# Hybrid encoder block on one core: the single unit's first step moved ahead of the second products, and the residual rows' transfers moved to ScalarE's queue

## The chip, the core and the metric

The kernel runs on one core of a Trainium2 chip. The metric is the time of one execution on the device in microseconds; the kernel before takes 1399.41 us, the median of 3 runs (1399.37 to 1400.16). Engine names are those of the profile: PE (TensorE, matmul) and PEld (its weight loads), DVE (VectorE), ACT (ScalarE), POOL (GpSimd) and SP (SyncE, which issues most DMAs); a q behind a name is the engine's sequencer, which issues DMAs and waits.

## The reference, cut to what matters

One encoder layer over 256 tokens of width 2048, everything in float32. Three attention mixers are merged by gates, projected by `w_o` and added to the residual; then comes a gated feed-forward layer of inner width 5632 with a second residual add:

```
h = rms_norm(x, g_mix);  proj = h @ w_in            # q, k, v of the mixers and three gates
...
merged = gates0 * (oa @ w_br_a) + gates1 * (ob @ w_br_b) + gates2 * (oc @ w_br_c)
x = x + merged @ w_o
hf = rms_norm(x, g_ffn) @ w_ffn_in                   # 2048 x 11264
x = x + (silu(hf[..., :D_FF]) * hf[..., D_FF:]) @ w_ffn_out
```

The change touches the `w_o` product, the feed-forward products and the last residual add.

## The kernel before, in words

**Tiling.** The 256 tokens are two halves of 128 rows (t = 0, 1). A weight matrix is cut into blocks of 256 input rows by 512 output columns, 512 KB each, stored so that a block is one DMA of 128 partitions x 1024 values. A float32 product is made from rounded parts: ACT copies a weight tile to the type that PE takes (`whi`, L444 in `halves`), DVE subtracts that from the original to get the remainder (`wlo`, L455 in `low`), and PE does three matmuls of 128x512 for each pair of tiles: high x high, high x low, low x high.

**Seven products instead of eight.** `pair` (L457) makes two neighbouring blocks of 512 output columns at once. Where it can, it takes a 2x2 group (two token halves or input blocks by two column blocks) and replaces its eight block products by seven with sums of blocks as operands. These seven are the steps X, W, P, Y, Q, Z, H, with a digit for the group; the sums of the activations are prepared tiles (`forms`, `lone`), the sums of the weights are made by accumulating DMAs on POOL (L545, L554, L560) or by DVE (L644, L646, L648; L577, L579, L581 for the single unit). Blocks outside such groups are the plain steps d (first column block) and D (second).

**Order.** The order of the steps is written by hand in the `STEPS_` lists (L54 to L65), one string for the front, one for the back and one for the tail of a pair; a "." in a front takes one step of the tail of the pair before. `run` (L681) calls each step's preparation (loads, DVE sums, `whi`, `wlo`) four steps ahead of its matmuls (`ahead` is 4), so that ACT and DVE stand four steps ahead of PE in program order. Letters l, r, a and s are not products: l0 and l1 start the two groups' first loads and the accumulating DMA into `t`; r0 and r1 load the block `b22` of group 0 or 1 (`begin2`, L547); s0 loads the two blocks of the single unit and sums into one of them (L557); a0 and a1 accumulate one more block into `t` (L553).

**Ends of phases.** All X steps of a pair add into one PSUM bank. After the last of them `phase_end` (L601) has ACT copy that bank into a new one for Y (L613); P, the next product, goes on adding into the X bank and so must wait for the copy. After the last W step ACT copies the W bank to `m5` (L616), and after the last P step DVE writes `m5` minus X into the W bank (L618). These copies are put on ACT and DVE in the order in which the products are called (`nc.follow`), that is behind the `whi` copies of the four steps that follow the step which ends the phase.

**The feed-forward pairs.** `feeding` (L1058) makes eleven pairs of `w_ffn` (n = 0 to 10), in three groups (0 to 3, 4 to 7, 8 to 10), each group followed by two pairs of `w_ffn_out`. Pair n = 0 uses `STEPS_FFN0`, the other ten use `STEPS_FFN5`. This list has two groups (0 and 1) and one single unit: S1 to S4 are a 2x2 group inside one input block, of half the width. S1 is half an X product and half a W product, so it belongs to both phases; S2 is P and Y, S3 Q and Z, S4 H. Its plain steps are D4, D5, D7 and d4, d5, d7; the three d steps are its tail and stand at the three "." of the next front.

**Places.** A loaded block goes to the first free place of one list (`free`, L212; 15 places from n = 1 on), and `release` puts a place at the end of that list after the step that uses the block. SP issues loads in program order, so a load waits until the place that it was given is free, and everything behind it on SP waits too.

**Residual rows.** In `projecting` (L997) DVE adds the `w_o` product to the residual rows `x` in SBUF (L1023), and `keep` (L1008) stores each finished block of 128 x 512 to the DRAM tile `held`: eight DMAs of 256 KB on SP, three ticks after the add. Pairs of `w_ffn_out` that aren't the last accumulate into `held` by POOL's DMAs (L1096). Before the last two pairs `rows_back` (L1052) loads `held` into two SBUF tiles `xb0` and `xb1`, two DMAs of 1 MB on SP, eight ticks after it is started; the last additions (L1103) write into these and `store` (L1048) sends them out from SP.

Of the kernel before, what the change touches and what calls it, by code (L numbers as in the profile page):

```python
# [25 lines left out]
NC = 512  # L26
# [32 lines left out]
STEPS_O2 = ("l0 X0 . r0 W0 . P0 Y0 . Q0 .", "Z0 D2 H0 D3 d2 D4 D5 d3 D6 D7", "d4 d5 d6 d7")  # L59
STEPS_FFN0 = ("l0 l1 X0 X1 . r0 W0 . r1 W1 . P0 P1 . Y0 Q0 Q1 Y1", "Z0 Z1 D6 H0 D7 H1 D4 D5", "d6 d7 d4 d5")  # L60
STEPS_FFN = ("l0 l1 X0 X1 . r0 W0 r1 W1 P0 P1 . Y0 Y1 . Q0 Q1 .", "Z0 Z1 D4 H0 D5 H1 D6 D7", "d4 d5 d6 d7")
STEPS_FFN5 = ("l0 l1 s0 X0 X1 . W0 W1 S1 r0 P0 . r1 P1 S2 Y0 Y1 . Q0 a0 Q1 a1 S3",
              "Z0 Z1 D4 H0 D5 H1 D7 S4", "d4 d5 d7")
STEPS_LAST = ("l0 l1 X0 X1 . r0 W0 . r1 W1 . P0 P1 . Y0 Q0 Q1 Y1", "Z0 Z1 H0 H1 D4 D5", "d4 d5")
STEPS_LAST2 = ("l0 l1 X0 X1 . r0 W0 r1 W1 P0 P1 . Y0 Q0 Q1 Y1", "Z0 Z1 D4 H0 D5 H1 d4 d5", "")  # L65
# [40 lines left out]
def encoder_block(ctx: ExitStack, tc: tile.TileContext, a: dict, out: bass.AP):  # L106
    nc = InOrder(tc)
# [13 lines left out]
    def s8(shape, name, dt=F32R, pool=None):  # L121
        return (pool or big).tile(shape, dt, name=name, tag="s8")

    def s4(shape, name, dt=F32):
        return mid.tile(shape, dt, name=name, tag="s4")
# [37 lines left out]
    def row_scale(ss, r):  # L163

        v = small.tile([P, T], F32, name="rs_v")
        nc.follow(nc.vector.tensor_scalar(v, ss, 1.0 / D, EPS, op0=ALU.mult, op1=ALU.add))
        y = []
        yield from root_of(v, [P, T], y)
        nc.follow(nc.vector.tensor_copy(r[:, 0], y[0]))
        nc.follow(nc.vector.tensor_mul(r[:, 1], y[0], y[0]))  # L170
# [14 lines left out]
    def start(steps):  # L185

        job = [0, steps]
        side.append(job)
        advance(job)
# [7 lines left out]
    def urgent(steps):  # L197

        while True:
            with tc.high_priority():  # L200
                try:
                    lag = next(steps)
                except StopIteration:
                    return
            yield lag
# [94 lines left out]
    def transposed(src, dst, g=None, lag=1, also=None, single=None):  # L300


        full = None
        for h in range(2):
            if h:
                yield lag
            tp = bank("tp", "tp")
            for k in range(2):
                for t in range(T):
                    nc.tensor.transpose(tp[:, k * S + t * P:k * S + (t + 1) * P],  # L310
                                        src[t][:, (2 * h + k) * P:(2 * h + k + 1) * P], ident)
            if g is None:
                d = dst(2 * h, 2)
                split(d[0], d[1], tp.rearrange("p (k s) -> p k s", s=S))
            else:
                for k in range(2):
                    d = dst(2 * h + k, 1)
                    split(d[0], d[1], tp[:, k * S:(k + 1) * S], g(2 * h + k))
            if also is not None:
                if full is None:  # L320
                    full = s4([P, 2, 4, P], "ffull")
                to, of = full[:, :, 2 * h:2 * h + 2], tp.rearrange("p (k t s) -> p k t s", t=T, s=P)
                if g is None:
                    nc.scalar.activation(to, of, AF.Copy)
                else:
                    for k in range(2):
                        nc.scalar.activation(to[:, k], of[:, k], AF.Copy, scale=g(2 * h + k))
            if single is not None and h == 0:
                one, of = s4([P, 1, 4, P], "ffull"), tp.rearrange("p (k s) -> p k s", s=S)
                for k in range(2):  # L330
                    nc.scalar.activation(one[:, 0, 2 * k:2 * k + 2].rearrange("p t s -> p (t s)"), of[:, k], AF.Copy,
                                         scale=g(k) if g else 1.0)
                token_sums(one, single)
        if also is not None:
            token_sums(full, also)
# [46 lines left out]
    def hold(n, steps):  # L382
        yield n
        yield from steps
# [554 lines left out]
    held = dram.tile([P, T, D], F32, name="held")  # L939
    mT, x1T, x, room, lone = {}, [], [], [], []  # L940
# [56 lines left out]
    def projecting():  # L997
        def rows():
            yield 16
            for t in range(T):  # L1000
                x.append(s8([P, D], f"x{t}", F32))
                nc.sync.dma_start(out=x[t], in_=a["x"][t * P:(t + 1) * P, :])
                yield 1
        start(rows())
        mTl = lambda k: (mT[k // 4][:, 0, k % 4], mT[k // 4][:, 1, k % 4])
        ended = []

        def keep(i, xc):  # L1008
            for t in range(T):
                nc.sync.dma_start(out=held[:, t, i * NC:(i + 1) * NC], in_=xc[t])  # L1010
            yield 1

        def root():
            yield 4
            ssr = small.tile([P, T], F32, name="ss", bufs=1)
            nc.follow(nc.vector.tensor_reduce(ssr, ss1, axis=AX.X, op=ALU.add))
            yield from row_scale(ssr, r_f)

        for n in (0, 2):
            def add(c, r, n=n):  # L1020
                xc = [x[t][:, (n + c) * NC:(n + c + 1) * NC] for t in range(T)]
                for t in range(T):
                    nc.vector.tensor_add(xc[t], r[t], xc[t])  # L1023
                start(hold(3, keep(n + c, xc)))
                ended.append(n + c)
                last = len(ended) == 4

                def later():
                    yield 1
                    sq = s4([P, T, NC], "sq")  # L1030
                    for t in range(T):
                        nc.scalar.activation(sq[:, t], xc[t], AF.Square, accum_out=ss1[:, t, n + c:n + c + 1])
                    if last:
                        start(urgent(root()))
                    yield 2
                    if not x1T:
                        x1T.extend(s8([P, 2, 4, S], "x1T") for _ in range(4))
                        room.extend(form_room(3))
                        lone.append(s4([P, 1, 2, 4, P], "lone", F32R))
                    yield from transposed(xc, lambda k, m: (x1T[n + c][:, 0, k], x1T[n + c][:, 1, k]),  # L1040
                                          lambda k: gT[:, 2, 4 * (n + c) + k:4 * (n + c) + k + 1], 2,
                                          also=room[2 + n + c] if n == 0 else None,
                                          single=lone[0] if n + c == 3 else None)
                start(urgent(later()))
            yield pair(block_pair(a["w_o"], n), mTl, STEPS_O2 if n else STEPS_O, add, TWO[:1], by_room(lambda: room))
# [6 lines left out]
    def rows_back():  # L1052
        x[:] = [s8([P, D], f"xb{t}", F32) for t in range(T)]
        for t in range(T):
            nc.sync.dma_start(out=x[t], in_=held[:, t])
            yield 1

    def feeding():  # L1058
        for c0, c1 in ((0, 4), (4, 8), (8, KF // 4)):
# [3 lines left out]
            for n in range(c0, c1):  # L1063
# [5 lines left out]
                def hidden(c, v, av=av, n=n - c0, hT=hT):  # L1069
# [8 lines left out]
                    def later():  # L1078
                        tl = hT[n] = s8([P, 2, 4, S], "hT", pool=home(n))
                        yield 3  # L1080
                        yield from transposed([av[0][:, t] for t in range(T)],
                                              lambda k, m: (tl[:, 0, k:k + m], tl[:, 1, k:k + m]), lag=2,
                                              also=room[n] if n < 2 else None)
                    start(urgent(later()))
                yield pair(lambda u, c, n=n: a["w_ffn"][n][2 * u + 1 - c], x1l, STEPS_FFN5 if n else STEPS_FFN0, hidden,
                           TWO, by_room(lambda: room[2:4]), single=(6, lambda f: [lone[0][:, 0, i, (f + 1) % 4] for i in range(2)]))
            pairs = (STEPS_LAST, STEPS_LAST2) if last else (STEPS_FFN, STEPS_FFN)
            if last:
                start(hold(8, rows_back()))
# [111 lines left out]
```

## Time and profile before

| | |
|---|---|
| median of 3 runs | 1399.41 us (1399.37 to 1400.16) |
| the profiled execution | 1397.66 us, of which its span is 1395.9 us |
| granted PE clock over the span | 0.99 |
| busy share of PE, DVE, ACT, POOL | 98%, 83%, 63%, 6% |
| mean DMA rate | 231 GB/s |
| DMA into and out of HBM | 312.37 MB read, 9.17 MB written |

Read it so: a busy share says how much of the span an engine was doing something, not that it ran at its best rate; the granted clock is the share of PE's full clock that the throttle allowed. The view of waits names, for an engine's idle time, which instruction ended it, with the total, the number of times and the longest. The timeline prints for each instruction its start, its duration, engine, line and tiles, and in brackets the idle time of its engine before it. Views by window give busy time, clock and DMA share of one stretch.

### The profile page before, as it was taken

To read this page: it belongs to the slowest core of one execution; us is meant where nothing else is said; L and a number is where in the kernel's file an instruction comes from. 1 tells how busy PE (TensorE), PEld (TensorE's weight loads), DVE (VectorE), ACT (ScalarE), POOL (GpSimd) and SP (SyncE) were. 2 spreads that over 40 slices of the span, in tenths; PEclk is the share of its full clock that TensorE was granted. 3 is DMA by queue.
4 is the path that set the end of the run, shared out by engine and by line. 5 is a ranking of instruction groups with operands and counts; after the bars stand their busy time and mean duration, and the time that the engine had idled before them with its cause. 6 is when DMAs were issued, how large, how long until landed. Compare 5 with 4: busy or idle time off the path is not lost. (4 is left out here: it accounts for less than half of the span.)

```text
span 1395.9 us, 17542 instructions
## 1 busy us (share of the span) xinstructions
PE 1361.7 (98%) x6146; PEld 1121.9 (80%) x6146; DVE 1161.0 (83%) x1460; ACT 885.1 (63%) x1181; POOL 88.2 (6%) x98
## 2 busy tenths in 40 slices
PE   9999999999999999999989999999999999999998
PEld 7888888888888888888767878878777888777877
DVE  6878877779977969867979898977898898878897
ACT  7876665655655656656656666666666666656664
POOL 0010000000000000000000100011100001110000
PEclk9999999999999999999999999999999999999999
DMA  9976445576668558738577976789876888887953
GB/s 372 336 237 207 137 162 168 165 218 196 239 193 300 196 181 294 235 134 294 182 247 257 288 201 214 251 253 289 259 209 230 270 256 263 209 269 232 336 160 107
DMA packets 94282, 322.71 MB, mean 231 GB/s; under 512 B 10545, under 2 KB 13105, under 8 KB 93681
## 3 DMA queue, kind: packets, MB, share of 16 engines
q1 hardware_dynamic: 80928, 280.14, 55.9%
q0 software_dynamic: 13120, 41.42, 16.2%
q8 instruction: 48, 0.79, 0.2%
q14 instruction: 42, 0.34, 0.1%
q10 hardware_dynamic: 144, 0.02, 0.0%
HBM read 312.37 MB, written 9.17 MB: 230 GB/s over the span
## 5 line engine op out<-in xcount | busy, mean ns | idle before, releaser
L444 ACT ACTIVATE whi<-raw 128x1024 fp32r<-128x1024 f32 (+1 forms) x320 | 316.3, 1000 | 200.3 <-PE mmQ L81 37.5
L455 DVE TENSOR_TENSOR wlo<-raw,whi 128x1024 fp32r<-128x1024 f32 (+1 forms) x320 | 364.7, 1150 | 86.8 <-ACT whi L444 84.2
L444 ACT ACTIVATE whi<-both 128x1024 fp32r<-128x1024 f32 (+1 forms) x195 | 194.5, 1006 | 118.6 <-DVE both L644 24.1
L455 DVE TENSOR_TENSOR wlo<-both,whi 128x1024 fp32r<-128x1024 f32 (+1 forms) x195 | 224.6, 1158 | 44.6 <-ACT whi L444 43.2
L81 PE MATMUL mm<-whi,xT 128*128 128x512 f32 x640 | 202.3, 393 | 0.0
L81 PE MATMUL mmX<-whi,forms 128*128 128x512 f32 x368 | 129.6, 407 | 25.4 <-ACT mmY L613 23.9
L81 PEld LDWEIGHTS mm<-whi,xT 128*128 128x128 f32 x640 | 119.2, 188 | 23.5 <-issue 0.4
L135 DVE TENSOR_TENSOR wlo<-raw,whi 128x1024 fp32r<-128x1024 f32 x82 | 103.2, 1261 | 36.9 <-ACT whi L134 36.4
L81 PE MATMUL mm<-wlo,xT 128*128 128x512 f32 x320 | 125.6, 393 | 0.0
L81 PE MATMUL mmW<-whi,forms 128*128 128x512 f32 x368 | 123.9, 392 | 0.0
L455 DVE TENSOR_TENSOR wlo<-more,whi 128x1024 fp32r<-128x1024 f32 (+1 forms) x88 | 103.6, 1178 | 23.7 <-ACT whi L444 22.9
L134 ACT ACTIVATE whi<-raw 128x1024 fp32r<-128x1024 f32 x82 | 86.8, 1062 | 56.0 <-PE mm L81 39.9
L81 PE MATMUL mmX<-whi,x1T 128*128 128x512 f32 x352 | 121.7, 390 | 0.0
L444 ACT ACTIVATE whi<-more 128x1024 fp32r<-128x1024 f32 (+1 forms) x88 | 89.8, 1022 | 43.6 <-PE mmQ L81 8.3
L81 PEld LDWEIGHTS mmX<-whi,forms 128*128 128x128 f32 x368 | 71.3, 194 | 45.1 <-ACT mmY L613 28.1
L81 PE MATMUL mmY<-whi,x1T 128*128 128x512 f32 x244 | 85.5, 407 | 0.2 <-ACT whi L444 0.2
L81 PEld LDWEIGHTS mmW<-whi,forms 128*128 128x128 f32 x368 | 69.1, 188 | 14.1
L81 PEld LDWEIGHTS mmX<-whi,x1T 128*128 128x128 f32 x352 | 66.5, 189 | 14.1
L81 PE MATMUL mmX<-wlo,forms 128*128 128x512 f32 x184 | 74.1, 403 | 0.0
L81 PE MATMUL mmW<-wlo,forms 128*128 128x512 f32 x184 | 71.8, 390 | 0.1
L81 PEld LDWEIGHTS mm<-wlo,xT 128*128 128x128 f32 x320 | 60.2, 188 | 12.4 <-issue 0.7
L81 PE MATMUL mmX<-wlo,x1T 128*128 128x512 f32 x176 | 68.8, 391 | 0.1
(315 smaller groups left out, 2631.1 us busy)
## 6 DMA issues: line engine op xcount, KB each, us to landing
raw<-in_w_ffn SPq DMA_DIRECT2D x85, 512.0 KB, 8.3
both<-in_w_ffn SPq DMA_DIRECT2D x67, 512.0 KB, 8.6
raw<-in_w_gate SPq DMA_DIRECT2D x66, 512.0 KB, 4.7
raw<-in_w_qkv SPq DMA_DIRECT2D x64, 512.0 KB, 4.3
raw<-in_w_ffn_out SPq DMA_DIRECT2D x42, 512.0 KB, 6.2
both<-in_w_ffn_out SPq DMA_DIRECT2D x35, 512.0 KB, 5.7
more<-in_w_ffn SPq DMA_DIRECT2D x24, 512.0 KB, 8.3
both<-in_w_ffn POOLq DMA_DIRECT2D x24, 512.0 KB, 8.7
```

The lines of the kernel that those rows point to most:

```text
L81: ins = op(*args, **kw)
L134: nc.scalar.activation(hi, src, AF.Copy)
L135: nc.vector.tensor_sub(lo, src, hi.bitcast(F32))
L444: nc.follow(nc.scalar.activation(hi[:, o], v, AF.Copy))
L455: nc.follow(nc.vector.tensor_sub(*part))
```

## The change

Two edits. In `STEPS_FFN5`, r0 and r1 move forward, right behind X0 and X1; S1 moves from behind W1 to the place ahead of W0; and the second "." (a tail step of the pair before) moves from behind P0 to between W0 and W1. In `keep` and `rows_back` the DMAs are issued by ACT instead of SP, in program order with the other followed instructions of ACT.

```
-STEPS_FFN5 = ("l0 l1 s0 X0 X1 . W0 W1 S1 r0 P0 . r1 P1 S2 Y0 Y1 . Q0 a0 Q1 a1 S3",
+STEPS_FFN5 = ("l0 l1 s0 X0 r0 X1 r1 . S1 W0 . W1 P0 P1 S2 Y0 Y1 . Q0 a0 Q1 a1 S3",
               "Z0 Z1 D4 H0 D5 H1 D7 S4", "d4 d5 d7")
...
         def keep(i, xc):
             for t in range(T):
-                nc.sync.dma_start(out=held[:, t, i * NC:(i + 1) * NC], in_=xc[t])
+                nc.follow(nc.scalar.dma_start(out=held[:, t, i * NC:(i + 1) * NC], in_=xc[t]))
...
         for t in range(T):
-            nc.sync.dma_start(out=x[t], in_=held[:, t])
+            nc.follow(nc.scalar.dma_start(out=x[t], in_=held[:, t]))
```

No arithmetic changes; the same matmuls, copies and DMAs are made. With the tail steps filled in, the products of a front that follows another `STEPS_FFN5` pair come in this order:

```
before: X0 X1 d4 W0 W1 S1 P0 d5 P1 S2 Y0 Y1 d7 Q0 Q1 S3
after:  X0 X1 d4 S1 W0 d5 W1 P0 P1 S2 Y0 Y1 d7 Q0 Q1 S3
```

## The prediction

> **What bounds the kernel now.** I read the page first, then the view of waits, then the timeline around one wait of the kind that leads it. The page's head and its first line say that PE is the bound:
>
> ```profile
> span 1395.9 us, 17542 instructions
> PE 1361.7 (98%) x6146; PEld 1121.9 (80%) x6146; DVE 1161.0 (83%) x1460; ACT 885.1 (63%) x1181; POOL 88.2 (6%) x98
> ```
>
> Only 1395.9 - 1361.7 = 34.2 us of PE are idle. The waits (total, times, longest) say where:
>
> ```profile
> PE mmX L81 <- ACT mmY L613: 23.9, 10, 5.0
> PE mmX L81 <- DVE mmW L618: 1.5, 1, 1.5
> ```
>
> One wait holds 23.9 us of the 34.2; the next is 1.5. Ten times is once for each `STEPS_FFN5` pair: P0 adds into the X bank and waits until ACT has copied that bank for Y. One of the ten, ACT's timeline first, then PE's:
>
> ```profile
> 1026.95 0.63 ACT L444 ACTIVATE whi<-both 128x512 fp32r<-128x512 f32 x1 [0.68 <-DVE both L577]
> 1027.49 0.61 ACT L444 ACTIVATE whi<-raw 128x512 fp32r<-128x512 f32 x1
> 1028.01 0.58 ACT L613 ACTIVATE mmY<-mmX 128x512 f32<-128x512 f32 x1
> ```
>
> ```profile
> 1026.13 0.39 PE L81 MATMUL mmW<-whi,lone 128*128 128x512 f32 x1
> 1028.64 0.77 PE L81 MATMUL mmX<-whi,forms 128*128 128x512 f32 x1 [2.12 <-ACT mmY L613]
> ...
> 1030.48 0.63 PE L81 MATMUL mmX<-wlo,forms 128*128 128x512 f32 x1
> 1030.91 0.63 PE L81 MATMUL mmX<-whi,forms 128*128 128x512 f32 x1
> ```
>
> PE had finished S1 at 1026.5. The copy takes 0.58 us but starts at 1028.01, because on ACT it stands behind the `whi` copies of four more steps, P0, d5, P1 and S2, and S2's wait for a DVE sum (L577). So PE doesn't wait for a busy ACT; it waits for a place in ACT's order. And the wait costs more than itself: behind it matmuls start 0.43 us apart (1030.48 to 1030.91). Windows of 5 us behind each of the ten waits (columns: PE, PEld, DVE, ACT, POOL busy, then the granted clock, DMA share, GB/s) show why:
>
> ```profile
> 719.70:724.70 5.00, 4.98 (x12) 3.92 (x13) 2.66 (x3) 2.47 (x3) 0.00 (x0) 0.50 0.31 107
> ...
> 1287.80:1292.80 5.00, 5.00 (x15) 3.97 (x16) 2.91 (x4) 2.46 (x3) 0.86 (x1) 0.66 0.44 105
> ```
>
> In seven of the ten the clock is below full: 0.50 once, 0.68 once, 0.66 five times; the other three show 1.00. Lost clock is 5.0 x (0.50 + 0.32 + 5 x 0.34) = 12.6 us. The waits thus cost 23.9 + 12.6 = 36.5 us, of which PE's busy share shows only the first part.
>
> **S1 ahead of W0.** This removes no work; what counts is what stands between S1 and P0 on PE, and on ACT ahead of the copy. Rows of the same pair, DVE and then PE:
>
> ```profile
> 1018.02 1.23 DVE L455 TENSOR_TENSOR wlo<-raw,whi 128x1024 fp32r<-128x1024 f32 x1
> 1019.17 1.22 DVE L455 TENSOR_TENSOR wlo<-both,whi 128x1024 fp32r<-128x1024 f32 x1
> 1020.30 1.22 DVE L644 TENSOR_TENSOR raw<-raw,more 128x1024 f32<-128x1024 f32 x1
> 1021.44 0.69 DVE L455 TENSOR_TENSOR wlo<-raw,whi 128x512 fp32r<-128x512 f32 x1
> ```
>
> ```profile
> 1022.28 0.39 PE L81 MATMUL mmW<-whi,forms 128*128 128x512 f32 x1
> ...
> 1023.64 0.39 PE L81 MATMUL mmW<-whi,forms 128*128 128x512 f32 x1
> ```
>
> A step of six matmuls takes PE 1023.64 - 1022.28 = 1.36 us, a plain step of twelve 2.72. In the new order S1 starts at 1022.28, its X half ends at about 1022.96, and behind it come W half 0.68, W0 1.36, d5 2.72, W1 1.36: P0 would start at 1029.1. The four steps behind S1 are now W0, d5, W1 and P0, so the copy stands behind P0's `whi`. DVE from 1018.02: two halves of S1 (0.60 each, 0.69 long with the overlap that the full ones show), W0 and d5 (1.14 each), P0's sum 1.14: 1022.6. ACT then copies P0's `whi` (1.06) and the X bank (0.58): 1024.3, 4.8 us ahead of P0. I therefore cost the wait at nothing. Its cover is these 6.1 us of PE work; without it the old 2.1 to 5 us are back. The W phase now ends with W1; its copy to `m5` goes behind Y0's `whi`, and its reader (L618) comes only after S2, as before.
>
> What is late next is DVE: three steps with sums (P0, P1, S2) now follow each other with no plain step between. From a window from one copy (L613) to the next:
>
> ```profile
> 982.90:1028.00 45.10, 43.00 (x185) 35.07 (x185) 39.82 (x45) 29.64 (x37) 4.34 (x5) 0.96 0.79 239
> ```
>
> ```profile
> 1008.00 1.23 DVE L455 TENSOR_TENSOR wlo<-raw,whi 128x1024 fp32r<-128x1024 f32 x1 [2.20 <-ACT whi L444]
> ```
>
> Without wait and clock loss PE needs 45.10 - 2.1 - 1.7 = 41.3 us for this interval; DVE is busy for 39.82 and sits 2.20 for H1's block, together 42.0: 0.7 short. Such tight intervals are four or five (those where the sums for `forms` are made as well), and DVE runs 2 to 3 us ahead of PE (below: 2.6), which absorbs most of it. I take 1 us in all, between 0 and 5 x 0.7 = 3.5.
>
> **r0 and r1 behind X0 and X1.** Two loads more stand on SP ahead of d4's, and one more ahead of d5's; S1's blocks are wanted two steps earlier. SP, then landing times by kind (count, KB, median us), then d4 on ACT, DVE and PE:
>
> ```profile
> 1000.09 0.33 SPq L81 DMA_DIRECT2D both<-in_w_ffn  x1
> 1001.23 0.33 SPq L81 DMA_DIRECT2D more<-in_w_ffn  x1
> 1002.36 2.06 SPq L81 DMA_DIRECT2D both<-in_w_ffn  x2
> ```
>
> ```profile
> both<-in_w_ffn SPq DMA_DIRECT2D x67, 512.0 KB, 8.6
> ```
>
> ```profile
> 1013.68 1.06 ACT L444 ACTIVATE whi<-both 128x1024 fp32r<-128x1024 f32 x1 [0.29 <-PE mmX L81]
> ...
> 1015.74 1.22 DVE L455 TENSOR_TENSOR wlo<-both,whi 128x1024 fp32r<-128x1024 f32 x1
> ...
> 1019.56 0.39 PE L81 MATMUL mmY<-whi,x1T 128*128 128x512 f32 x1
> ```
>
> These issues are d4 (1000.09), r0 (1001.23), then d5 and r1 (1002.36 and behind). d4 becomes the third: 1002.36 instead of 1000.09, 2.3 us later. Landing 0.33 + 8.6 later, at 1011.3, it is still 2.4 us ahead of ACT's use at 1013.68, and `wlo` has another 1019.56 - 1016.96 = 2.6 us before PE. Cover 5.0 us: nothing, in most pairs. Not so where loads are late already:
>
> ```profile
> 704.68 1.06 ACT L444 ACTIVATE whi<-raw 128x1024 fp32r<-128x1024 f32 x1 [5.19 <-DMA raw<-in_w_ffn]
> ```
>
> ```profile
> 938.00:983.00 45.00, 43.13 (x189) 35.39 (x189) 36.51 (x38) 28.65 (x35) 5.51 (x6) 1.00 0.89 262
> ```
>
> In the pair n = 1 ACT waits 5.19 us for the tail step d6, and this load falls behind r0 and r1: 2.3 us more, taken in full (0 to 4.6). Behind the first pair of each later group (n = 5, n = 9) the DMA share is 0.89 against 0.79; I take 1 us in each (0 to 2.5). What remains is 1 + 2.3 + 2 = 5.3 us.
>
> **Stores and loads through ACT.**
>
> ```profile
> SPq L81 <- DVE x L1023: 66.6, 8, 21.9
> ```
>
> ```profile
> 570.00:661.00 91.00, 91.00 (x418) 75.30 (x417) 71.23 (x80) 56.75 (x80) 2.58 (x3) 1.00 0.67 231
> ```
>
> ```profile
> 0.74 0.40 ACTq L349 DMA_DIRECT2D gT<-in_g_rows  x1
> ```
>
> The eight stores block SP for 66.6 us until the rows are added, and the weight loads behind them. But in that stage PE is busy for 91.00 of 91 us, so earlier loads win nothing. ACT issues a DMA in 0.40 us (its only one); eight make 3.2 us, in a stage where it is idle for 34 of 91. The added wait, for the add, is queued ahead of ACT's `whi`; the store stands three ticks behind the add, and ACT's squares (L1032) already wait for the same rows, so I cost it at nothing (0 to 8 x 0.4, or -1 where three loads of n = 0 come sooner). `rows_back`:
>
> ```profile
> 1310.60 0.80 SPq L81 DMA_DIRECT2D xb<-held  x2
> ```
>
> ```profile
> 1355.73 0.35 DVE xb L1103
> ```
>
> SP issued them at 1310.60 without any wait; ACT reaches them eight steps (of 1.36 to 2.72 us) later, by my estimate around 1328; even at twice the 8.6 us of a block half as large they land by 1346, 10 us ahead of the first use. Nothing either way.
>
> **Sum.** 36.5 - 5.3 = 31.2 us less. The profiled execution (1397.66, span 1395.9) would be at 1366.5; the median stands 1.75 above it, so 1399.41 - 31.2 = 1368.2.
>
> [...] The rows say that a PE wait of 2.1 us was followed by half clock in this pair. [...]
>
> **Rivals.** *DVE becomes the bound.* For it: 39.82 of 45.10 busy, and of its 5.28 idle only 2.20 is H1's. If another 1.0 of the other 3.08 stays, an interval takes 43.0, 2.1 less than now: ten give 21, so 1378. Against: DVE's lead of 2.6 us, and the intervals without `forms`, in which it can win it back. Chance 0.15. *Nothing moves*, the copy being late behind P0's sum after all: 1399.4. Against: 4.8 us of room. 0.03. *The slow clock stays*: 23.9 - 5.3 = 18.6 less, 1380.8. For it: three waits of the ten have no slow clock behind them; against: seven have, at once. 0.03. *d4's load stops ACT in every pair*, slower: a pair wins 36.5 / 10 = 3.65, so from a landing 5.0 + 3.65 = 8.65 us later than worked out (17.3 us from issue) it loses. At 19 us PE waits 5.4 and the clock costs 1.26 again, 3.0 more than now in each pair: 1429. Against: 8.6 is the median. 0.04.
>
> **How the numbers follow.** The forecast has 0.75. Low end: no residue, and some us of the 34.2 - 23.9 others besides: 1360. High end: the DVE rival with the upper residues of the late loads (5.3 more), 1384; left out are no change, slower, and the worst of the others. A difference under 0.2% (2.8 us) can't be told from none: faster 0.93, same 0.03, slower 0.04.
>
> **What would show it.** Right: PE's wait for L613 gone from the list, no half clock between 715 and 1295, copies 41 to 42 us apart, d6 of n = 1 later on ACT. Wrong: PE waiting for `wlo` (L455) for more than 1 us at P1, S2 or Y0; ACT waiting for `in_w_ffn` at d4; ACT idle ahead of its own DMA issues.

## The result and the profile after

The changed kernel takes 1383.28 us, the median of four runs (1382.37 to 1384.77); the kernel before took 1399.39 us beside it. The ratio is 0.9889, with a 95% interval of 0.9872 to 0.9906. The forecast was 1368.2: the time moved the way it said, by 16.1 us instead of 31.2. The profiled execution took 1383.93 us, of which the span is 1382.2. The head of its page and the first line:

```profile
span 1382.2 us, 17556 instructions
PE 1357.3 (98%) x6146; PEld 1113.1 (81%) x6146; DVE 1157.9 (84%) x1460; ACT 878.1 (64%) x1181; POOL 88.1 (6%) x98
```

PE is idle for 1382.2 - 1357.3 = 24.9 us, 9.3 less than before. Its busy time fell by only 4.4 us, although the granted clock over the span rose from 0.990 to 0.998. PE's waits (total, times, longest):

```profile
PE mmX L81 <- DVE wlo L455: 8.4, 9, 1.3
PE mmW L81 <- DVE wlo L455: 5.3, 11, 0.7
PE mmX L81 <- DVE mmW L618: 2.6, 2, 1.5
PE mmY L81 <- DVE wlo L455: 1.6, 4, 0.8
```

The wait for L613, 23.9 us before, is gone from the list. In its place PE waits for low halves: 8.4 + 5.3 + 1.6 = 15.3 us in 24 short waits, where the kernel before had 2.8 us in five (0.7, 0.9 and 1.2 in the same three rows). The copy itself, on ACT, and the first matmul of P0, on PE, in the pair n = 6:

```profile
1014.90 1.06 ACT L444 ACTIVATE whi<-raw 128x1024 fp32r<-128x1024 f32 x1 [2.69 <-DVE raw L644]
1015.87 0.58 ACT L613 ACTIVATE mmY<-mmX 128x512 f32<-128x512 f32 x1
```

```profile
1019.40 0.39 PE L81 MATMUL mmX<-whi,forms 128*128 128x512 f32 x1
```

The copy ends at 1016.45, 2.95 us ahead of P0 (4.8 were forecast); it stands behind P0's `whi`, as worked out. From one copy to the next (columns: PE, PEld, DVE, ACT, POOL busy, then granted clock, DMA share, GB/s):

```profile
972.50:1015.90 43.40, 41.90 (x184) 33.17 (x183) 39.52 (x45) 28.72 (x38) 4.34 (x5) 1.00 0.84 252
1015.90:1059.60 43.70, 41.78 (x187) 33.73 (x186) 39.50 (x45) 28.78 (x37) 4.32 (x5) 1.00 0.84 246
```

The clock is full, but the interval is 43.4 to 43.7 us where 41 to 42 were forecast. DVE is busy for 39.5 of it (39.8 before). Where its other 4.2 us went, on ACT and then on DVE, in the second of these windows:

```profile
1042.84 1.06 ACT L444 ACTIVATE whi<-more 128x1024 fp32r<-128x1024 f32 x1 [6.22 <-DMA more<-in_w_ffn]
```

```profile
1038.76 1.21 DVE L455 TENSOR_TENSOR wlo<-raw,whi 128x1024 fp32r<-128x1024 f32 x1
1043.93 1.23 DVE L455 TENSOR_TENSOR wlo<-more,whi 128x1024 fp32r<-128x1024 f32 x1 [3.96 <-ACT whi L444]
```

This is H1: ACT waits 6.22 us for the block that a1 accumulates, and DVE 3.96 us for ACT, nearly all of DVE's idle time in this window. The same instruction in the kernel before:

```profile
1052.86 1.22 DVE L455 TENSOR_TENSOR wlo<-both,whi 128x1024 fp32r<-128x1024 f32 x1 [1.96 <-ACT whi L444]
```

Added up over the ten `STEPS_FFN5` pairs, DVE's idle time ahead of H1's low half was 17.2 us before (0.13 to 4.51 each) and is 30.5 after (0.52 to 4.26): 13.3 us more.

**The round that sets the interval.** After Q1's sum (L646), which still reads the block `t`, a1 may be issued on POOL; its landing lets ACT make H1's `whi`, then DVE makes H1's low half, and then comes all DVE work up to the next Q1 sum. POOL's rows for the pair n = 6, after and then before:

```profile
1029.27 0.86 POOL L545 DMA_DIRECT2D both<-in_w_ffn  x1 [2.92 <-ACT whi L444]
1029.81 1.21 POOL L554 DMA_DIRECT2D more<-in_w_ffn  x1
```

```profile
1038.99 0.86 POOL L545 DMA_DIRECT2D raw<-in_w_ffn  x1 [2.76 <-DMA raw<-in_w_ffn]
1039.53 1.21 POOL L554 DMA_DIRECT2D both<-in_w_ffn  x1
```

L545 is the accumulating load of the next pair's l1, L554 is a1, right behind it on the same queue in both kernels. After the change a1 lands at 1042.7, 12.9 us after its issue; before it took 12.1. The view of line L554, before and then after (a0 and a1 together):

```profile
  ACT whi L444: 31.3, 11
...
DMA to landing us min/median/max: 5.4/10.6/13.8
```

```profile
  ACT whi L444: 55.9, 16
...
DMA to landing us min/median/max: 8.3/12.1/14.2
```

Over the ten a1 loads the time from issue to landing adds up to 118.7 us before (10.3 to 13.8 each) and 131.9 after (12.6 to 14.2), 13.2 us more; their issue comes 1.3 us later behind Q1's sum, in all. So nearly all of DVE's 13.3 us come from the longer landing, not from a later issue. The traces' records of issue and landing say where it is longer. In both kernels a1 lands 3.6 to 4.7 us after the last of the DMAs that were issued ahead of it. The time from a1's issue until that last one has landed adds up to 79.7 us before and 92.2 after, 12.5 us more. The growth is in the loads that are still on their way when a1 is issued.

### The profile page after: what moved, and what is told of

The parts are those of the page before. It is cut to its first block, busy times and chain, and to the rows that moved or that the text cites. A ratio compares the mean times of both kernels' runs of the same rounds, so it can differ in the third digit from the quotient of the medians.

```text
span 1382.2 us, 17556 instructions
## 1 busy us (share of the span) xinstructions
PE 1357.3 (98%) x6146; PEld 1113.1 (81%) x6146; DVE 1157.9 (84%) x1460; ACT 878.1 (64%) x1181; POOL 88.1 (6%) x98
## 4 chain that ended last, share of the span: by engine, by line
PE 71%; DVE 13%; DMA 11%; issue 3%; ACT 3%; POOL 0%; SPq 0%; ACTq 0%; DVEq 0%; POOLq 0%
PE mmX L81 19%; PE mm L81 16%; PE mmW L81 14%; PE mmY L81 10%; PE mmQ L81 8%; DVE wlo L455 8%; DMA both<-in_w_ffn 7%; ACT whi L444 2%; DMA more<-in_w_ffn 2%; DVE raw L646 1%; PE o L81 1%; PE sc L81 1%; DMA raw<-in_w_ffn_out 1%; DVE both L646 1%; PE tp L81 1%
## 5 line engine op out<-in xcount | busy, mean ns | idle before, releaser
L444 ACT ACTIVATE whi<-both 128x1024 fp32r<-128x1024 f32 (+1 forms) x194 | 190.5, 992 | 110.6 <-DMA both<-in_w_ffn 34.0
L455 DVE TENSOR_TENSOR wlo<-both,whi 128x1024 fp32r<-128x1024 f32 (+1 forms) x194 | 220.2, 1141 | 40.6 <-ACT whi L444 39.7
L81 PE MATMUL mmX<-whi,forms 128*128 128x512 f32 x368 | 123.4, 395 | 2.6 <-DVE mmW L618 2.6
L134 ACT ACTIVATE whi<-raw 128x1024 fp32r<-128x1024 f32 x82 | 86.8, 1061 | 57.8 <-PE mm L81 41.3
L81 PE MATMUL mmY<-whi,x1T 128*128 128x512 f32 x244 | 81.5, 390 | 0.3 <-ACT whi L444 0.3
```

What stands on the lines that cost most here:

```text
L81: ins = op(*args, **kw)
L134: nc.scalar.activation(hi, src, AF.Copy)
L444: nc.follow(nc.scalar.activation(hi[:, o], v, AF.Copy))
L455: nc.follow(nc.vector.tensor_sub(*part))
```

## The experiments

Theory A: the round over a1's landing sets the interval, so the gain went into H1's wait. Rivals: DVE's work as a whole sets it, wherever it stands; the moved transfers cost it; or nothing in particular does. Each diff is against the changed kernel except where it says otherwise, and each ratio is against the kernel before, timed on the same chip. The changed kernel's is 0.9889; a ratio lower by 0.001 is 1.4 us.

**The two parts of the change, each alone.** First the new order with the residual rows on SP as before:

```
-                nc.follow(nc.scalar.dma_start(out=held[:, t, i * NC:(i + 1) * NC], in_=xc[t]))
+                nc.sync.dma_start(out=held[:, t, i * NC:(i + 1) * NC], in_=xc[t])
...
-            nc.follow(nc.scalar.dma_start(out=x[t], in_=held[:, t]))
+            nc.sync.dma_start(out=x[t], in_=held[:, t])
```

> The changed kernel with the stores and loads of the residual rows back on SP; only the order of the steps is changed. Theory A (what is left is DVE: 39.5 us of work an interval plus about 4 us in which it waits for H1's block, the accumulating DMA a1): the two queues play no part, so 1383 us, within 3 of the changed kernel, and ACT waits 5 to 6 us for H1's block as there. Rival C (ACT pays for issuing the residual DMAs): 5 to 10 us faster than the changed kernel, 1373 to 1378.

Measured: 1385.73 us (1384.93 to 1387.28), ratio 0.9922 (0.9906 to 0.9939). Then the reverse of this diff put into the kernel before:

> The kernel before with only the residual rows' DMAs on ACT. Theory A: nothing is gained or lost where PE is full, 1399 us within 3, with the ten waits for L613 as before. Rival C: slower than the kernel before by 5 to 10 us, 1404 to 1409.

Measured: 1396.66 us (1393.28 to 1399.89), ratio 0.9986 (0.9972 to 1.0). The order makes nearly all of the gain. The queue part gives about 2 us by itself, which its interval (up to 1.0) does not tell from none, and 2.5 (by the ratios 4.6) with the new order. One place where it shows: from the copy of n = 0 to that of n = 1 the time is 57.3 us with SP and 54.5 with ACT (54.5 to 56.5 in the other kernels with this front and ACT's queue), and ACT's wait for d6 of n = 1 is 7.92 us with SP and 5.99 with ACT. SP's 66.6 us of waits for the added rows (67.5 in the order-only run) are gone with ACT's queue, so a likely reason is that the loads of n = 0 no longer stand behind the stores; no run separates this.

**H1 behind D7.** H1 gets the 2.7 us of D7's matmuls more:

```
-               "Z0 Z1 D4 H0 D5 H1 D7 S4", "d4 d5 d7")
+               "Z0 Z1 D4 H0 D5 D7 H1 S4", "d4 d5 d7")
```

> The changed kernel with H1 one step later, behind D7. Theory A: DVE does D7's remainder (1.14 us) and its neighbours inside the wait for a1, so the interval shrinks by 1.1 to 2.3 us in eight of the ten pairs: 9 to 18 us faster than the changed kernel, 1365 to 1374, and DVE's idle time ahead of H1's remainder falls from 4 to 2 us or less. Rival B (r0 and r1 ahead of d4's load are what is lost): no difference, 1383 within 3.

Measured: 1371.53 us (1371.31 to 1373.7), ratio 0.9822 (0.9807 to 0.9836), 9 us (by the ratios) to 12 us (by the medians) less than the changed kernel. From copy to copy, the same two intervals:

```profile
969.92:1011.17 41.25, 40.82 (x184) 33.48 (x183) 39.71 (x45) 28.82 (x38) 4.34 (x5) 1.00 0.87 268
1011.17:1052.99 41.82, 41.36 (x186) 33.93 (x186) 39.82 (x45) 28.75 (x38) 4.32 (x5) 1.00 0.85 258
```

These are close to the 41.3 us that the prediction gave as PE's need. The work is the same (DVE 39.7 to 39.8); only the idle time went: 9.1 us ahead of H1 in ten pairs, instead of 30.5. The rows also show that PE's busy share hides part of such a loss: the same 184 matmuls at full clock count as 41.90 us busy in the changed kernel and as 40.82 here.

**r0 and r1 back at the second products.**

```
-STEPS_FFN5 = ("l0 l1 s0 X0 r0 X1 r1 . S1 W0 . W1 P0 P1 S2 Y0 Y1 . Q0 a0 Q1 a1 S3",
+STEPS_FFN5 = ("l0 l1 s0 X0 X1 . S1 W0 . W1 r0 P0 r1 P1 S2 Y0 Y1 . Q0 a0 Q1 a1 S3",
```

> The changed kernel with r0 and r1 back to right ahead of P0 and P1; S1 stays ahead of W0. Theory A: a1 lands no sooner, 1383 us within 3. Rival B: d4's load has its 2.3 us back, and up to 8 us are won: 1375.

Measured: 1379.18 us (1376.72 to 1379.87), ratio 0.987 (0.9855 to 0.9884), 3 to 4 us less than the changed kernel, though the two intervals overlap. H1's idle time is the same (29.9 us), so this is another loss. It stands in the front behind the first pair of a group, here d4 of n = 4 on ACT in the changed kernel:

```profile
963.64 1.06 ACT L444 ACTIVATE whi<-both 128x1024 fp32r<-128x1024 f32 x1 [4.37 <-DMA both<-in_w_ffn]
```

With r0 and r1 back, ACT does not wait there, and the interval to the copy of n = 5 is 43.0 us instead of 45.9. The next one is 44.4 instead of 43.4, so a third of it is given back, by this account to H1's round. The fronts behind n = 0 and n = 8 show the same with 1.4 and 4 us.

**Both.**

```
-STEPS_FFN5 = ("l0 l1 s0 X0 r0 X1 r1 . S1 W0 . W1 P0 P1 S2 Y0 Y1 . Q0 a0 Q1 a1 S3",
-               "Z0 Z1 D4 H0 D5 H1 D7 S4", "d4 d5 d7")
+STEPS_FFN5 = ("l0 l1 s0 X0 X1 . S1 W0 . W1 r0 P0 r1 P1 S2 Y0 Y1 . Q0 a0 Q1 a1 S3",
+               "Z0 Z1 D4 H0 D5 D7 H1 S4", "d4 d5 d7")
```

> The changed kernel with two edits of its step list together: H1 behind D7, and r0/r1 back at the second products. Theory A (two separate losses: DVE stands idle at H1 until the late sum of a1 has landed, in every pair, and the d4 load, issued behind r0 and r1, lands late in the first pair after an output pair): the two gains add up, 1383.3 - 12 - 4 = 1367 us, 1364 to 1370. Theory B (one loss seen at two places: whichever is mended first takes the same idle time): 1370 to 1373, no better than H1 late alone.

Measured: 1373.39 us (1369.72 to 1374.32), ratio 0.9813 (0.9797 to 0.9829): not to be told from H1 late alone. The gains did not add up, and theory A was wrong to say so. The interval to the copy of n = 5 falls from 46.0 to 42.9 us, but the next rises from 41.25 to 42.38: what one place wins, the round over a1 takes back in part.

**One DVE instruction more, at two places.** This tells theory A from "DVE's work in all". In P0, behind H1:

```
                 hi, lo = halves(raw)
+                if ns and kind + str(m) == "P0":
+                    due[-1].append(due[-1][-1])
```

> The changed kernel with one DVE instruction more in each of the ten pairs of STEPS_FFN5: the low half of P0 is computed twice (1.14 us, same result). P0 stands behind H1 of the pair before and ahead of the Q1 sum. Theory A (the round from the Q1 sum over the load a1 to H1's low half and on to the next Q1 sum sets the interval): it counts in full, 1383.3 + 10 x 1.14 less what the first pair of each group absorbs, 1389 to 1395. Theory B (DVE's work in all sets the interval, wherever it stands): the same here, 1390 to 1395. Theory C (DVE does not set it; PE's small waits are bursts that any order has): 1382 to 1386.

Measured: 1399.12 us (1395.56 to 1401.73), ratio 0.9998 (0.9985 to 1.001), 15 to 16 us more than the changed kernel and above both expected ranges. The intervals grew by what the instruction takes:

```profile
980.37:1025.01 44.64, 42.25 (x184) 33.17 (x184) 40.77 (x46) 28.82 (x38) 4.32 (x5) 1.00 0.81 241
1025.01:1069.88 44.87, 42.64 (x187) 33.56 (x186) 40.78 (x46) 28.92 (x38) 4.33 (x5) 1.00 0.81 240
```

That is 1.24 and 1.17 us more. From the first copy to the last the growth is 14.9 us; the interval with the late d4 has the largest part, 2.9. Then the same in D5, ahead of H1, as I thought:

```
                 release(raw)
+                if ns and (u, c) == (5, 1):
+                    due[-1].append(due[-1][-1])
```

> The changed kernel with the same instruction more, but in D5, just ahead of H1's low half, where DVE stands idle for 3 to 5 us. Theory A (the round over a1's landing sets the interval): it is done in the idle time and costs nothing, 1381 to 1386. Theory B (DVE's work in all sets the interval): as in P0, 1390 to 1395. Theory C: 1382 to 1386.

Measured: 1409.82 us (1408.55 to 1412.92), ratio 1.0081 (1.0066 to 1.0097): slower than every expectation. The DVE rows say why:

```profile
1003.11 1.21 DVE L455 TENSOR_TENSOR wlo<-raw,whi 128x1024 fp32r<-128x1024 f32 x1
1008.33 0.69 DVE L135 TENSOR_TENSOR hT<-tp,hT 128x512 fp32r<-128x512 f32 x1 [4.00 <-ACT hT L134]
1008.93 1.22 DVE L455 TENSOR_TENSOR wlo<-raw,whi 128x1024 fp32r<-128x1024 f32 x1
```

The second low half was put behind an `hT` subtraction, which needs ACT's `hT`; that stands on ACT behind H1's `whi`, and so behind a1's landing. D5's products then waited for H1's load:

```profile
PE mmW L81 <- DVE wlo L455: 26.0, 12, 3.7
```

So this run does not answer the question it was made for. It shows how an instruction that costs 1.14 us turns into PE waits of up to 3.7 us where it lands behind a wait: 26.0 us in all. The repeat is in Z0, behind Q1's sum and ahead of H1, where the order of DVE stays as it was:

```
                 hi, lo = halves(raw)
+                if ns and kind + str(m) == "Z0":
+                    due[-1].append(due[-1][-1])
```

> The changed kernel with the low half of Z0 computed twice in each of the ten pairs: the same 1.14 us of DVE as in P0, but behind the Q1 sum and ahead of H1, and with the instructions of DVE otherwise in the order of the changed kernel (in D5 the second low half was put behind a copy that waits for ScalarE, so that run does not answer the question). Theory A (the round over a1's landing sets the interval): done in the idle time, 1382 to 1387. Theory B (DVE's work in all sets it, wherever it stands): as in P0, 1394 to 1399.

Measured: 1384.11 us (1383.85 to 1386.69), ratio 0.9906 (0.9884 to 0.9928). DVE does the same work as with P0's, and the intervals stay:

```profile
972.86:1016.38 43.52, 41.93 (x184) 33.17 (x184) 40.77 (x46) 28.75 (x37) 4.34 (x5) 1.00 0.84 250
1016.38:1059.60 43.22, 41.84 (x187) 33.78 (x186) 40.78 (x46) 28.72 (x37) 4.32 (x5) 1.00 0.84 249
```

```profile
1033.53 2.48 DVE L455 TENSOR_TENSOR wlo<-more,whi 128x1024 fp32r<-128x1024 f32 x2
...
1043.92 1.23 DVE L455 TENSOR_TENSOR wlo<-more,whi 128x1024 fp32r<-128x1024 f32 x1 [2.17 <-ACT whi L444]
```

H1's low half starts at 1043.92, against 1043.93 without the extra work: it was done in the idle time. Over the ten pairs DVE's idle time ahead of H1 falls to 20.9 us, where with P0's it is 36.9. With 40.77 us of DVE work in both, one kernel needs 44.6 to 44.9 us a pair and the other 43.2 to 43.5. That is theory A's answer, and the rival is out.

**l1 later.** Where the next pair is a `STEPS_FFN5` pair too, and l1's accumulating load stands right ahead of a1 on POOL's queue, this takes it away; s0's, half as large, then stands there. By POOL's rows these are four of the ten pairs (n = 2, 5, 6 and 9):

```
-STEPS_FFN5 = ("l0 l1 s0 X0 r0 X1 r1 . S1 W0 . W1 P0 P1 S2 Y0 Y1 . Q0 a0 Q1 a1 S3",
+STEPS_FFN5 = ("l0 s0 X0 l1 r0 X1 r1 . S1 W0 . W1 P0 P1 S2 Y0 Y1 . Q0 a0 Q1 a1 S3",
```

> The changed kernel with l1 (and so its accumulating load on POOL) behind X0 in place of ahead of s0. If the later issue of a1 behind l1's accumulate on POOL is what lengthened H1's wait (theory A1): a1 is issued up to 1.2 us sooner in each pair, 1373 to 1380. If it is the fuller transfer queues that let a1 land later (theory A2), or l1 then comes too late for W1's sum: 1381 to 1387.

Measured: 1375.1 us (1374.77 to 1376.27), ratio 0.9833 (0.9816 to 0.9849), 8 us less. The size is A1's, the way is not. In this kernel a1 is issued 1.6 us later over the ten pairs, but lands sooner:

```profile
DMA to landing us min/median/max: 7.9/10.7/14.3
```

Over the ten a1 loads that is 123.7 us instead of 131.9, 8.2 less, and 7.7 of it in the four pairs where the order on POOL's queue changed. DVE's idle time ahead of H1 falls by 7.1 us, to 23.4.

**H1 and l1 late, and all three.** First the two list edits for l1 and H1 together, then r0 and r1 back as well:

```
-STEPS_FFN5 = ("l0 l1 s0 X0 r0 X1 r1 . S1 W0 . W1 P0 P1 S2 Y0 Y1 . Q0 a0 Q1 a1 S3",
-               "Z0 Z1 D4 H0 D5 H1 D7 S4", "d4 d5 d7")
+STEPS_FFN5 = ("l0 s0 X0 l1 r0 X1 r1 . S1 W0 . W1 P0 P1 S2 Y0 Y1 . Q0 a0 Q1 a1 S3",
+               "Z0 Z1 D4 H0 D5 D7 H1 S4", "d4 d5 d7")
```

```
-STEPS_FFN5 = ("l0 l1 s0 X0 r0 X1 r1 . S1 W0 . W1 P0 P1 S2 Y0 Y1 . Q0 a0 Q1 a1 S3",
-               "Z0 Z1 D4 H0 D5 H1 D7 S4", "d4 d5 d7")
+STEPS_FFN5 = ("l0 s0 X0 l1 X1 . S1 W0 . W1 r0 P0 r1 P1 S2 Y0 Y1 . Q0 a0 Q1 a1 S3",
+               "Z0 Z1 D4 H0 D5 D7 H1 S4", "d4 d5 d7")
```

> The changed kernel with H1 behind D7 and l1 behind X0. Theory A: each alone takes time from the same idle stretch at H1 (12 and 8 us), and PE's own 41.3 us a pair is the floor that H1 late already reaches in the second pair of each group, so together little more than H1 late alone: 1368 to 1373 us. Theory B (two separate losses): 1361 to 1366.

> All three: H1 behind D7, l1 behind X0, r0 and r1 back at the second products. With no idle time at H1 and no late d4 load, PE's work should set the end in every pair: 1364 to 1370 us by theory A (the floor is PE's 41.3 us a pair, the rest of the loss stands outside these pairs). If moving l1 makes W1's or H1's loads late in their turn: 1371 to 1377.

Measured: 1368.03 us (1367.9 to 1369.53), ratio 0.9789 (0.9768 to 0.981), and 1365.03 us (1363.58 to 1366.37), ratio 0.9766 (0.9744 to 0.9787). The last beats both kernels, the one before by 32 us. Its page:

```profile
span 1362.5 us, 17559 instructions
PE 1347.8 (99%) x6146; PEld 1114.2 (82%) x6146; DVE 1159.6 (85%) x1460; ACT 879.2 (65%) x1181; POOL 88.1 (6%) x98
```

Both lie in theory A's ranges. In the last PE is idle for 14.7 us, against 24.9 in the changed kernel and 34.2 before. DVE's idle time ahead of H1 is 7.4 us in ten pairs.

**S1 two steps ahead instead of three.** Only S1 moves; r0, r1 and d5 stand where they stood before, and the residual rows go through ACT's queue:

```
-STEPS_FFN5 = ("l0 l1 s0 X0 r0 X1 r1 . S1 W0 . W1 P0 P1 S2 Y0 Y1 . Q0 a0 Q1 a1 S3",
+STEPS_FFN5 = ("l0 l1 s0 X0 X1 . S1 W0 W1 r0 P0 . r1 P1 S2 Y0 Y1 . Q0 a0 Q1 a1 S3",
```

> The smallest edit of the list that moves S1: only S1 ahead of W0, r0, r1 and d5 where they were in the kernel before, the residual rows through ScalarE's queue. S1 then stands two steps ahead of P0 in place of three. By the prediction's room of 4.8 us less d5's 2.7 us, 2.1 us are left, so the copy still holds nothing up and PE's wait at it stays away: 1376 to 1383 us (as with r0 and r1 back). If three steps are needed: part of the 23.9 us of waits and the half clock are back, 1385 to 1395.

Measured: 1393.0 us (1390.64 to 1398.53), ratio 0.9978 (0.9962 to 0.9993). The time is that of the second case, its cause is not: PE's wait for L613 is absent here too, so two steps are enough for the copy. But DVE idles ahead of H1 for 47.6 us in ten pairs. POOL's rows, then DVE's:

```profile
980.96 0.86 POOL L554 DMA_DIRECT2D both<-in_w_ffn  x1 [1.20 <-DVE both L646]
989.18 0.86 POOL L545 DMA_DIRECT2D both<-in_w_ffn  x1 [7.36 <-DMA both<-in_w_ffn]
989.72 1.21 POOL L554 DMA_DIRECT2D raw<-in_w_ffn  x1
```

```profile
982.31 1.22 DVE L646 TENSOR_TENSOR raw<-raw,raw 128x1024 f32<-128x1024 f32 x1
...
1002.41 1.23 DVE L455 TENSOR_TENSOR wlo<-raw,whi 128x1024 fp32r<-128x1024 f32 x1 [6.12 <-ACT whi L444]
```

Q1's sum ends at 983.5, but a1 is issued at 989.72: on POOL it stands behind l1's accumulating load, which waits for its own block to land. Here the later issue, 6.2 us, is the loss. That the same round loses by the landing in one order and by the issue in another is a second sign, beside the spare instruction in P0 and in Z0, that it is the round that counts.

## Why the prediction fell short, point by point

The forecast was 15.1 us too low.

**The wait and its clock, 36.5 us.** Right. PE's wait for L613 is gone in every kernel with S1 ahead of W0, and the granted clock is 1.00 in both windows shown. In the run with all three edits PE's idle time is 19.5 us and its busy time 13.9 us less than before, near the 23.9 and 12.6 of the sum, so time of that size was there. The copy's room came out at 2.95 us where 4.8 were worked out, and was enough. Nine of the ten waits before are 1.66 to 2.45 us long; the longest is the 5.0 us, and the clock behind it is the 0.50.

**r0 and r1, 4.3 us.** Right in total, as far as the noise lets one say: 3 to 4 us, in the fronts behind the first pair of a group. The parts differ: 1.4, 2.9 and 4 us at the three places where 2.3, 1 and 1 were put down, some of it taken back in the intervals behind them.

**The queue, nothing.** Undersized: 2 to 4.6 us, probably for the reason named as "-1 where three loads of n = 0 come sooner".

**DVE, "I take 1 us in all, between 0 and 5 x 0.7 = 3.5".** This step failed. It took H1's 2.20 us from the profile of before as a constant and let DVE's lead absorb the rest. But the 2.20 is what is left of a landing time after the DVE work that fits beside it, and the landing changed: DMA share 0.84 instead of 0.79 in these windows, a1's landing 13.2 us longer in all, H1's idle time 13.3 us longer. And a lead can't absorb a wait that comes back in each pair in a round that DVE closes itself. What the term measured: H1 behind D7, which takes 21.4 us of DVE's idle time away, gives back 9 to 12 us, where 1, at most 3.5, was put down. With l1 late as well the kernel takes 1368.03 us, beside the 1368.2 forecast, so the other terms of the sum hold together; that the two numbers meet so closely is in part luck, since l1's move was no part of the sum. The rival "DVE becomes the bound", chance 0.15, is what happened, with a wrong place: it let 1.0 of the other 3.08 us of idle time stay and H1's 2.20 as they were. Of those 3.08 only 0.24 stayed (4.20 - 3.96 in the second window); H1's own wait grew instead. That its interval of 43.0 lies near the 43.4 to 43.7 measured, and its 1378 near 1383, is therefore luck in part.

**The marks named.** L613 gone, no half clock between 715 and 1295: seen. d6 of n = 1 later on ACT: seen, by 0.8 us. Copies 41 to 42 us apart: not seen. ACT waiting at d4: seen, but only behind the first pairs. PE waiting for `wlo` for over 1 us at P1, S2 or Y0: not there; the longest, 1.3 us, stand at Q1.

**a1's landing.** The view of L554 after shows 12.1 us at the median for 512 KB; the shortest landing of L554 in the two kernels is 5.4 us. Most of a1's landing is the time until the DMAs issued ahead of it have landed (92.2 of 131.9 us in the changed kernel), and it changes with the order of the other loads (12.1 to 10.7 us in the view of L554 when only l1 moved).

What stays open: why more is still on its way when a1 is issued. A closer crowd of loads once PE no longer stalls would fit the DMA share of 0.84, but the other runs speak against it as the whole reason: with P0's low half twice the interval is nearly as long as before the change (44.6 to 44.9 us, share 0.81), and the ten landings add up to 133.1 us; with H1 late the share is 0.85 to 0.87 and they add up to 129.5. With r0 and r1 back they are 129.3, so these two loads are not it either. Of l1's accumulating load it is shown: taking it from right ahead of a1 took 8.2 us back. But it stood there before the change too.

## What to carry to other kernels

When a stall on the busiest engine is removed, look for the rounds that close over several engines (sum, accumulating load, copy, subtraction, next sum) and add up each round's whole length, landing included; the longest one is the next bound, whatever the busy shares say. An idle time that the profile shows in such a round is a remainder, not a constant: it must be worked out anew for the new order. And a spare instruction put once inside and once outside the suspected wait tells in two runs whether that wait sets the pace, if the order of the engine's other instructions stays as it was.

## What was not expected of the hardware

Half clock does not follow the length of PE's wait alone. In the changed kernel a wait of 1.54 us, in the part ahead of the changed pairs, was followed by it:

```profile
681.52 0.64 PE L81 MATMUL mmX<-whi,forms 128*128 128x512 f32 x1 [1.54 <-DVE mmW L618]
```

```profile
681.50:686.50 5.00, 4.98 (x15) 3.98 (x16) 5.00 (x6) 3.82 (x6) 0.00 (x0) 0.66 0.97 271
```

The same wait in the kernel before, 1.53 us, was not:

```profile
682.00 0.47 PE L81 MATMUL mmX<-whi,forms 128*128 128x512 f32 x1 [1.53 <-DVE mmW L618]
```

```profile
682.00:687.00 5.00, 5.00 (x24) 4.17 (x25) 5.00 (x6) 3.53 (x5) 0.00 (x0) 1.00 0.98 382
```

In the run with D5's low half twice, a wait of 3.74 us (ending at 1010.20) was followed by half clock and one of 3.08 us (ending at 1058.08) was not:

```profile
1010.20:1015.20 5.00, 5.00 (x12) 3.98 (x13) 5.00 (x6) 1.59 (x3) 0.00 (x0) 0.50 0.94 320
1058.10:1063.10 5.00, 5.00 (x22) 4.16 (x23) 5.00 (x6) 3.22 (x4) 0.00 (x0) 1.00 0.95 344
```

The trace of the kernel before has seven stretches of half clock ahead of the kernel's end: six of 3.41 us, and one of 6.83 at the 5.0 us wait. By my estimate a stretch costs half its length, 1.7 or 3.4 us. They start at 718.08, 769.28, 813.65, 984.32, 1028.69, 1243.73 and 1288.11 us, which are 15, 13, 50, 13, 63 and 13 times 3.413 us apart. The one in the changed kernel starts at 681.66 us and takes 3.41. Below are windows of 3.41 us, two that end at the first and the sixth of the seven starts, then three that lie whole multiples of 3.413 us from those and hold the longest part of each of the three waits for L613 without half clock:

```profile
714.67:718.08 3.41, 0.03 (x1) 0.00 (x0) 3.41 (x5) 1.17 (x3) 0.00 (x0) 1.00 0.07 29
1240.32:1243.73 3.41, 1.43 (x6) 1.21 (x7) 2.52 (x4) 3.09 (x5) 0.00 (x0) 1.00 0.46 154
936.53:939.94 3.41, 1.75 (x8) 1.41 (x8) 2.51 (x4) 3.09 (x5) 0.00 (x0) 1.00 0.49 154
1069.65:1073.07 3.42, 1.97 (x9) 1.31 (x7) 3.42 (x5) 2.08 (x3) 0.00 (x0) 1.00 0.08 8
1195.94:1199.35 3.41, 2.30 (x10) 1.92 (x11) 2.51 (x4) 3.08 (x6) 0.00 (x0) 1.00 0.42 144
```

Ahead of the seven starts PE is idle for 1.98 to 3.38 us of such a window, and for 1.84 ahead of the one in the changed kernel; in the three others it is idle for 1.66, 1.45 and 1.11 us. That is what these two traces show; what sets the half clock off was not shown.
